# The third block of four FFN heads put into a hand-written order, with the gates moved behind the last product's splits

## The chip, the cores and the metric

The kernel runs on one core of one Trainium2 chip. The metric is the device time of one launch in microseconds (us). TensorE is PE in the profile (PEld is its weight load), VectorE is DVE, ScalarE is ACT, GpSimd is POOL, SyncE is SP. SP and POOL issue the DMAs.

## The reference

A trunk of four layers over one sequence of 512 positions and 1024 channels, all in fp32. Each layer is a mixer (S5, gated linear attention, differential attention, S5) and a SwiGLU feed-forward network (FFN), and all four FFNs have the same shape:

```python
DEPTH, D_MODEL, FFN_HIDDEN = 4, 1024, 2816
for layer in range(DEPTH):
    h = rmsnorm(x, norm_mix[layer])
    x = x + mixer(h)                      # s5, gla, diff attention, s5
    h = rmsnorm(x, norm_ffn[layer])
    g, u = split(h @ ffn_w_gate_up[layer], 2)
    x = x + (silu(g) * u) @ ffn_w_down[layer]
return rmsnorm(x, norm_final)
```

## The kernel before

**Products.** Every fp32 number is split into a high part (a cast to fp32r on ScalarE) and a low part (a subtraction on VectorE), and a product is three matmul passes: high times high, high times low, low times high. The first two matmuls of a product therefore need a low part of only one operand or of none; the third needs the low part of the weights (`seven_product`, L583 to L595). A weight piece of 512 x 256 is loaded as one DMA of 512 KB, cast by `high` (L420) and subtracted by `low` (L428).

**Blocks.** The gate and up projection of an FFN is cut into eleven blocks of 256 columns (`seven_block`, L729). A block is a 2 x 2 Strassen-like scheme with seven products of 24 matmuls each, called `one`, `two`, `three`, `four`, `five`, `six`, `seven`. Its weight pieces are named after quarters of the weight: `11`, `21`, `22`, `1` (the sum of two quarters; the second is added by an accumulating DMA on GpSimd, L759) and `3` (another such sum, the step `summed`). `add22` and `add21` (L817) add the piece 22, then 21, onto piece 1 in place; the results are called S (for `six`) and F (for `four`), and `highS`, `lowS`, `highF`, `lowF` split them. The row side (the normalised activations) has pieces of its own, formed by `total1` to `total4` (L223, L227) and split by `high1` to `high4`, `high22` and `low1` to `low22` (L236, L241).

**Outputs of a block.** `one_out`, `five_out`, `six_out` copy a PSUM bank on ScalarE; `two_out` (L803), `seven_out` (L838) and `three_out` (L845, L846) combine on VectorE. `gate1` multiplies the first half of the gate by the norm factor (L768, VectorE) and applies silu (L769, ScalarE). `four_out` does the same for the second half in a tile `g2`, multiplies it with the up half (L855) and splits both halves of the finished activation into high (L865, ScalarE) and low (L866, VectorE). Buffers: four PSUM banks for the products `a` and `c` of all blocks together, two for `d`; three buffers for the tiles `r5`, `r2`, `g2` together; three staging buffers `wst` for pieces 11 and 3 and for the pieces of w_down; five buffers `whl` for split weights.

**Order.** The instructions are traced in the order of the Python code, and a scheduler at build time arranges each engine's queue: among those that it thinks ready it takes the one traced first, and a tile's buffer is given out again only when all readers of the old tile are placed. Between `hand_all()` and `hand()` the instructions of PE, ACT, DVE, SP and POOL keep the written order among themselves; instructions traced later may still be put between them.

**The head of an FFN.** The last part of the mixer's output projection runs under `hand_all()`. The first two blocks (called a and b here, as in the code) then follow a plan, a string of steps in which `one:a` is a product or an output of a block, `add21a` or `lowFa` a step on weights, and `total3`, `high4`, `low22` a step on the row side. `planned` (L711) runs it. Layer two has a plan of its own: there the step `turn` writes x to DRAM and reads it back in another order, by four DMAs on GpSimd (L984, L986, L988, L990). After the plan `hand()` ends the written order. Then come `four_out` of a and b, then the third block (c): its five loads (`direct` for piece 11, `room1`, `room22`, `room21`, `summed`; SP, and POOL for the two sums), `one`, `five`, `add22`, `six`, and so on, left to the scheduler. Layer two traces c's loads and the split of its piece 1 ahead of `four_out` of a, and its `one` and `five` ahead of `four_out` of b. In layer 0 three blocks, in the others four, are followed by the first product with w_down (`gemm_b`, L452, matmuls L448 to L450).

In the mixer of layer two (`diff`) the last half of the output projection is written by hand too; `between` (L2779) says what is put behind which k of which row tile t. The row side's piece 3 (`total("3")`, two subtractions at L223) is formed there in the plan of layer two, right behind `one:b`; for the other layers it is formed earlier, in the mixer.

Of the kernel before, what the change touches and what calls it, by code (L numbers as in the profile page):

```python
# [17 lines left out]
ALU = mybir.AluOpType  # L18
# [7 lines left out]
NT = SEQ // P  # L26
# [314 lines left out]
class Trunk:  # L341
# [369 lines left out]
    def planned(self, plan, left, f, more):  # L711

        for step in plan.split():
            name, _, n = step.partition(":")
            if n:
                f["ab".index(n)][name]()
            elif name in more:
                more[name]()
            elif name[-1] in "ab":
                word = next(w for w in ("split", "add", "high", "low") if name.startswith(w))  # L720
                w = name[len(word) : -1]
                f["ab".index(name[-1])][word]({"S": "1", "F": "1"}.get(w, w))
            elif name in ("finish", "diag", "spread", "rows"):
                getattr(left, name)()
            else:
                word = next(w for w in ("total", "high", "low") if name.startswith(w))
                getattr(left, word)(name[len(word) :])

    def seven_block(self, fp, slots, left, wgu, b, turn, na):  # L729
# [3 lines left out]
        v = nc.vector  # L733
# [117 lines left out]

        def four_out():
            g2 = T("g2")
            scaled(g2, bank["a"], 1)
            v.tensor_tensor(keep["r5"][:], g2[:], keep["r5"][:], op=ALU.mult)  # L855
            act = fp.tile([P, 2, 2, SEQ], F32R, tag="act", name="act", bufs=na)
# [13 lines left out]
            high, low, split, direct, room21, room1, room22, summed, one, one_out, two, two_out, gate1, five, five_out,  # L870
            add, six, six_out, seven, seven_out, three, three_out, four, four_out,
        )}

    def ffn(self, l, left, after=None, turn=False, aside=None, small=None):
# [5 lines left out]
        nxt = None  # L880
        r = left.r
        with self.tc.tile_pool(name=f"ffn{l}", bufs=1, reuse_waits="tile") as fp:
# [12 lines left out]
            blocks = [self.seven_block(fp, slots, left, wgu, b, turn, na) for b in range(FFN_HIDDEN // 256)]  # L895
            f = blocks[:2]
            if glued:
# [28 lines left out]

            self.planned(plan, left, f, {"square": lambda: left.square(NT - 1, 1), "flush": self.flush, "turn": turned})
            self.hand()
            F = left.freed()
            if aside:  # L930

                self.jobs = aside(Slices(left.whole, left.g))
            else:

                self.jobs = small() if small else iter(())
                slots[:] = [F[0], F[1], slots[0], F[2], left.g[:].rearrange("p (k n) -> p k n", n=256), F[3]] + slots[1:]
            b0 = 0
            for nb in (4, 4, 3) if na == 4 else (3, 3, 3, 2):
                acts = []
                for n in range(b0, b0 + nb):  # L940
                    b = blocks[n]
                    third = l == 2 and n < 3
                    loads = lambda b: [b[w]() for w in ("direct", "room1", "room22", "room21", "summed")]
# [1537 lines left out]
    def diff(self, l, left, after):  # L2481
# [4 lines left out]
        with self.tc.tile_pool(name="diff", bufs=1) as p:  # L2486
# [289 lines left out]
            for t in range(2):  # L2776
# [73 lines left out]
```

## Time and profile before

| | |
|---|---|
| median of 3 runs | 2236.42 us (2235.76 to 2239.88) |
| profiled execution: its time | 2237.47 us |
| profiled execution: its span, first to last instruction | 2235.8 us |
| granted TensorE clock, mean | 0.998 |
| busy share of the span | PE 97%, PEld 88%, DVE 73%, ACT 51%, POOL 15% |
| DMA, mean rate | 149 GB/s |
| FFN heads in the trace (first `one:a`) | 207, 781, 1394 and 1891 us |

A row of the timeline gives the start, the duration, engine, line, operation, the tile written and the tiles read, partitions x elements, how many instructions were merged, and in brackets the idle time of the engine just before and what ended it. A product of 24 matmuls shows as one row `x24`; `x2` and `x22` are the two parts of one that waited before its third matmul. Matmul rows overlap, so a product is timed from start to start.

### The profile page before, as it was taken

Reading aid. Unit: us, or ns where it says so; the run is one execution under the profiler, and the core shown is the slowest. Engines: PE = TensorE matmul, PEld = TensorE weight load, DVE = VectorE, ACT = ScalarE, POOL = GpSimd, SP = SyncE. Lnnn points to the kernel's source line nnn. Section 1 sums busy time; section 2 is a strip of 40 time slices with the busy share of each in tenths; the row PEclk is TensorE's granted clock in tenths of the full one; section 3 lists DMA queues with packets and bytes.
Section 4 is the critical chain, followed back from the end, with each engine's and each line's share of the span. In section 5 each row is a group of like instructions: output and inputs, shape, how many; then the busy total and the mean of one; then the engine's idle time right before and its main releaser. Section 6 shows DMA issues by size and latency. Waiting matters only on the chain.

```text
span 2235.8 us, 38463 instructions
## 1 busy us (share of the span) xinstructions
PE 2172.6 (97%) x15433; PEld 1969.9 (88%) x15433; DVE 1629.2 (73%) x2497; ACT 1141.6 (51%) x1835; POOL 330.1 (15%) x441
## 2 busy tenths in 40 slices
PE   6999899999999999999999999999999999999998
PEld 5888889989988899999988888999998888989997
DVE  9965878777978597876745676967766965957675
ACT  8644535444655465564435776644544234635343
POOL 3401152430211010100002221200000001101000
PEclk9999999999999999999999999999999999999999
DMA  4357667764863576765337455975631646866532
GB/s 92 64 172 178 175 153 183 182 172 150 188 148 105 153 182 179 179 180 138 98 129 165 99 142 143 248 203 137 185 95 48 170 142 151 201 157 167 163 76 76
DMA packets 309181, 333.63 MB, mean 149 GB/s; under 512 B 70477, under 2 KB 253033, under 8 KB 308874
## 3 DMA queue, kind: packets, MB, share of 16 engines
q1 hardware_dynamic: 238970, 238.93, 35.0%
q0 software_dynamic: 70032, 92.23, 21.9%
q8 instruction: 122, 2.00, 0.4%
q14 instruction: 57, 0.47, 0.1%
HBM read 297.16 MB, written 18.75 MB: 141 GB/s over the span
## 4 chain that ended last, share of the span: by engine, by line
PE 81%; DVE 9%; ACT 4%; issue 3%; DMA 1%; SPq 1%; POOL 0%; DVEq 0%; POOLq 0%; ACTq 0%
PE a L594 20%; PE acc L448 11%; PE acc L450 11%; PE acc L449 11%; PE c L594 10%; PE d L594 5%; DVE whl L428 2%; PE y L1634 2%; PE acc L1670 2%; ACT whl L420 1%; PE op L2633 1%; PE s L2600 1%; PE tp L117 1%; PE V L1590 1%; PE acc L2688 1%
## 5 line engine op out<-in xcount | busy, mean ns | idle before, releaser
L428 DVE TENSOR_TENSOR whl<-wst,whl 128x1024 fp32r<-128x1024 f32 x260 | 316.7, 1223 | 219.9 <-ACT whl L420 216.8
L594 PE MATMUL a<-side,whl 128*128 128x256 f32 x3240 | 392.6, 277 | 6.5 <-DVE whl L428 6.3
L420 ACT CAST whl<-wst 128x1024 fp32r<-128x1024 f32 x260 | 272.1, 1051 | 244.5 <-PE acc L450 152.7
L594 PEld LDWEIGHTS a<-side,whl 128*128 128x128 f32 x3240 | 379.2, 188 | 8.7 <-DVE whl L428 7.4
L448 PE MATMUL acc<-whl,act 128*128 128x512 f32 x704 | 275.8, 392 | 3.1 <-DVE g L768 3.1
L449 PE MATMUL acc<-whl,act 128*128 128x512 f32 x704 | 274.4, 390 | 0.0
L450 PE MATMUL acc<-whl,act 128*128 128x512 f32 x704 | 274.4, 390 | 0.0
L594 PE MATMUL c<-side,whl 128*128 128x256 f32 x2160 | 261.4, 277 | 3.8 <-DVE whl L428 3.8
L594 PEld LDWEIGHTS c<-side,whl 128*128 128x128 f32 x2160 | 253.1, 188 | 4.7 <-DVE whl L428 4.6
L428 DVE TENSOR_TENSOR whl<-slot,whl 128x1024 fp32r<-128x1024 f32 x105 | 127.7, 1222 | 60.7 <-ACT whl L420 60.2
L448 PEld LDWEIGHTS acc<-whl,act 128*128 128x128 f32 x704 | 132.1, 188 | 31.5 <-DVE g L768 3.5
L450 PEld LDWEIGHTS acc<-whl,act 128*128 128x128 f32 x704 | 132.1, 188 | 27.8
L449 PEld LDWEIGHTS acc<-whl,act 128*128 128x128 f32 x704 | 132.2, 188 | 26.3
L420 ACT CAST whl<-slot 128x1024 fp32r<-128x1024 f32 x105 | 109.9, 1053 | 86.3 <-PE acc L450 46.3
L594 PE MATMUL d<-sides,whl 128*128 128x256 f32 x1080 | 132.4, 278 | 2.6 <-ACT whl L420 2.6
L594 PE MATMUL a<-sides,whl 128*128 128x256 f32 x1080 | 132.3, 278 | 2.2 <-DVE whl L428 1.2
L594 PEld LDWEIGHTS d<-sides,whl 128*128 128x128 f32 x1080 | 128.0, 188 | 3.4 <-ACT whl L420 3.4
L594 PEld LDWEIGHTS a<-sides,whl 128*128 128x128 f32 x1080 | 127.9, 188 | 3.5 <-DVE whl L428 1.4
L428 DVE TENSOR_TENSOR whl<-halves,whl 128x1024 fp32r<-128x1024 f32 x87 | 105.9, 1221 | 32.1 <-ACT whl L420 31.8
L420 ACT CAST whl<-halves 128x1024 fp32r<-128x1024 f32 x87 | 91.0, 1052 | 71.6 <-DVE halves L817 24.9
L759 POOL DMA_DIRECT2D wst<-in_ffn_w_gate_up_dram x44 | 57.1, 1297 | 453.3 <-DMA wst<-in_ffn_w_gate_up_dram 167.5
L865 ACT CAST act<-r 128x512 fp32r<-128x512 f32 (+1 forms) x110 | 66.2, 643 | 107.7 <-DVE r L846 85.7
(511 smaller groups left out, 4028.9 us busy)
## 6 DMA issues: line engine op xcount, KB each, us to landing
wst<-in_ffn_w_gate_up_dram SPq DMA_DIRECT2D x88, 512.0 KB, 4.7
wst<-in_ffn_w_down_dram SPq DMA_DIRECT2D x88, 512.0 KB, 4.6
slot<-in_ffn_w_gate_up_dram SPq DMA_DIRECT2D x69, 512.0 KB, 6.3
wst<-in_ffn_w_gate_up_dram POOLq DMA_DIRECT2D x44, 512.0 KB, 6.0
halves<-in_ffn_w_gate_up_dram SPq DMA_DIRECT2D x42, 512.0 KB, 6.1
wst<-in_s_w_glu_dram SPq DMA_DIRECT2D x32, 512.0 KB, 4.9
wst<-in_diff_w_qkv_dram SPq DMA_DIRECT2D x24, 512.0 KB, 4.7
slot<-in_ffn_w_gate_up_dram POOLq DMA_DIRECT2D x18, 512.0 KB, 9.1
```

Source lines behind the costliest of these rows:

```text
L117: tr.nc.tensor.transpose(p[:, j], h[:, j * P : (j + 1) * P], tr.ident[:])
L420: self.last["high"] = self.nc.scalar.copy(hl[:, 0], w[:])
L428: self.last["low"] = self.nc.vector.tensor_tensor(hl[:, 1], w[:], hl[:, 0].bitcast(F32), op=ALU.subtract)
L448: mm(out, lh, rh, start=first, stop=False)
L449: mm(out, lh, rl, start=False, stop=False)
L450: self.last["mm"] = mm(out, ll, rh, start=False, stop=last)
L594: mm(o, *two, start=first and not (j or k or n), stop=k == 3 and n == 2, skip_group_check=True,)
L759: nc.gpsimd.dma_start(w[:], left.quarter(*plus, b), accum_op=ALU.add)
L865: self.last["act high"] = nc.scalar.copy(dst[:, 0, j], src[:, j])
L1590: mm(V[kk][z][:, bs(b)], inm[:, z, bs(b)], U[:, bs(b)], start=True, stop=True)
L1634: mm(yb[:, b], q[:, j, b], om[:, j // 2, bs(b)], start=False, stop=j == 3)
L1670: mm(accs[t][:], zT[:, m // 2, kk, t * P : (t + 1) * P], hl[:, m % 2, kk % 2], start=kk == 0 and m == 0, stop=kk == KT - 1 and m == 2,)
```

## The change

Four edits, all of them to the order:

1. In the plan of layers 0, 1 and 3 the splits for `four` (`high22`, `add21`, `low22`, `highF`, `lowF`) come ahead of the gates; `gate1:a` now follows `add21b` and `highFb`, and `gate1:b` and both `three_out` leave the plan. In layer two's plan `gate1:b` and both `three_out` leave too.
2. A second plan for all layers, still in the written order: the loads and first products of block c, with the outputs of a and b between them. `hand()` comes behind it. `four_out` becomes three steps: `gate2`, `times` and `parts`; `parts` (the splits of the finished activation) is traced after that plan.
3. The special case of layer two for block c is gone.
4. `total3` leaves layer two's plan; it is formed in `diff`, behind k = 3 of the last row tile.

No instruction is added or removed.

```diff
@@ planned
-                f["ab".index(n)][name]()
+                f["abc".index(n)][name]()
@@ seven_block
-        def four_out():
-            g2 = T("g2")
-            scaled(g2, bank["a"], 1)
-            v.tensor_tensor(keep["r5"][:], g2[:], keep["r5"][:], op=ALU.mult)
+        def gate2():
+            keep["g2"] = T("g2")
+            scaled(keep["g2"], bank["a"], 1)
+
+        def times():
+            v.tensor_tensor(keep["r5"][:], keep["g2"][:], keep["r5"][:], op=ALU.mult)
+
+        def parts():
             act = fp.tile([P, 2, 2, SEQ], F32R, tag="act", name="act", bufs=na)
...
@@ ffn
-            f = blocks[:2]
+            f = blocks[:3]
...
             if l == 2:
                 plan = """
-                    split21a one:a split21b square flush one:b total3 total1 one_out:a finish high1 low1 total2 split1a
+                    split21a one:a split21b square flush one:b total1 one_out:a finish high1 low1 total2 split1a
...
-                    high22 low22 three:a add21a highFa add21b lowFa highFb three:b lowFb seven_out:b gate1:a four:a gate1:b
-                    four:b three_out:a three_out:b
+                    high22 low22 three:a add21a highFa add21b lowFa highFb three:b lowFb seven_out:b gate1:a four:a
+                    four:b
                 """
             else:
...
-                    six_out:b total4 split22a high4 low4 seven:b seven_out:a split22b three:a seven_out:b gate1:a gate1:b
-                    add21a high22 low22 three:b highFa add21b lowFa highFb lowFb four:a four:b three_out:a three_out:b
+                    six_out:b total4 split22a high4 low4 seven:b seven_out:a split22b three:a seven_out:b high22 add21a
+                    low22 highFa lowFa three:b add21b highFb gate1:a lowFb four:a four:b
                 """
...
+            def loads(b=blocks[2]):
+                for w in ("direct", "room1", "room22", "room21", "summed"):
+                    b[w]()
...
-            self.hand()
             F = left.freed()
...
+            plan = """
+                loads split11c three_out:a split1c one:c gate2:a one_out:c five:c add22c highSc times:a gate1:b lowSc
+                five_out:c three_out:b gate2:b times:b
+            """
+            self.planned(plan, left, f, more)
+            self.hand()
...
-                    third = l == 2 and n < 3
...
-                    if third and n == 0:
-                        loads(blocks[2])
-                        blocks[2]["split"]("1")
-                    if third and n == 1:
-                        for step in ("one", "one_out", "five", "five_out"):
-                            blocks[2][step]()
-                        blocks[2]["add"]("22")
-                        blocks[2]["split"]("1")
-                    if n > 1 and not third:
+                    if n > 2:
...
-                        b["four"]()
-                    acts.append(b["four_out"]())
+                        for step in ("four", "gate2", "times"):
+                            b[step]()
+                    acts.append(b["parts"]())
@@ diff
-                3: {1: (one,), 3: (one,), 5: (one,)},
+                3: {1: (one,), 3: (one, lambda: nxt[0].total("3")), 5: (one,)},
```

More of the change, by code (lines that the diff above doesn't have):

```diff
@@ L715, in planned @@
             if n:
-                f["ab".index(n)][name]()
+                f["abc".index(n)][name]()
             elif name in more:
                 more[name]()
-            elif name[-1] in "ab":
+            elif name[-1] in "abc":
                 word = next(w for w in ("split", "add", "high", "low") if name.startswith(w))
                 w = name[len(word) : -1]
-                f["ab".index(name[-1])][word]({"S": "1", "F": "1"}.get(w, w))
+                f["abc".index(name[-1])][word]({"S": "1", "F": "1"}.get(w, w))
             elif name in ("finish", "diag", "spread", "rows"):
@@ L870, in seven_block @@
             high, low, split, direct, room21, room1, room22, summed, one, one_out, two, two_out, gate1, five, five_out,
-            add, six, six_out, seven, seven_out, three, three_out, four, four_out,
+            add, six, six_out, seven, seven_out, three, three_out, four, gate2, times, parts,
         )}
@@ L925, in turned @@
                 r = self.turn_x(left.r) if turn else r
-            self.planned(plan, left, f, {"square": lambda: left.square(NT - 1, 1), "flush": self.flush, "turn": turned})
-            self.hand()
+            def loads(b=blocks[2]):
+                for w in ("direct", "room1", "room22", "room21", "summed"):
+                    b[w]()
+            more = {"square": lambda: left.square(NT - 1, 1), "flush": self.flush, "turn": turned, "loads": loads}
+            self.planned(plan, left, f, more)
             F = left.freed()
@@ L936, in ffn @@
                 slots[:] = [F[0], F[1], slots[0], F[2], left.g[:].rearrange("p (k n) -> p k n", n=256), F[3]] + slots[1:]
+            plan = """
+                loads split11c three_out:a split1c one:c gate2:a one_out:c five:c add22c highSc times:a gate1:b lowSc
+                five_out:c three_out:b gate2:b times:b
+            """
+            self.planned(plan, left, f, more)
+            self.hand()
             b0 = 0
```

1 line of the change is left out of this document (removed).

## The prediction

> **What bounds the kernel now.** I read the page first: the busy shares, then the chain that ended last.
>
> ```profile
> PE 2172.6 (97%) x15433; PEld 1969.9 (88%) x15433; DVE 1629.2 (73%) x2497; ACT 1141.6 (51%) x1835; POOL 330.1 (15%) x441
> PE 81%; DVE 9%; ACT 4%; issue 3%; DMA 1%; SPq 1%; POOL 0%; DVEq 0%; POOLq 0%; ACTq 0%
> ```
>
> TensorE has work nearly all the time, so an edit that only reorders can give no more than the idle time of PE that it removes. Next I read PE's timeline through the four FFN heads. Layer one's, from the first matmul of `four:a`:
>
> ```profile
> 815.21 0.39 PE L594 MATMUL a<-side,whl 128*128 128x256 f32 x2
> 817.34 5.50 PE L594 MATMUL a<-side,whl 128*128 128x256 f32 x46 [1.74 <-DVE whl L428]
> 822.67 2.88 PE L594 MATMUL a<-sides,whl 128*128 128x256 f32 x24
> ...
> 826.89 2.78 PE L594 MATMUL c<-side,whl 128*128 128x256 f32 x22 [1.11 <-DVE whl L428]
> ...
> 830.66 0.50 PE L594 MATMUL d<-sides,whl 128*128 128x256 f32 x2 [0.44 <-ACT whl L420]
> 831.00 2.84 PE L594 MATMUL a<-side,whl 128*128 128x256 f32 x22
> 833.67 2.73 PE L594 MATMUL d<-sides,whl 128*128 128x256 f32 x22
> 836.24 2.88 PE L594 MATMUL a<-side,whl 128*128 128x256 f32 x24
> 838.96 2.88 PE L594 MATMUL c<-side,whl 128*128 128x256 f32 x24
> ```
>
> A product that waits for nothing takes 838.96 - 836.24 = 2.72 us (0.1133 a matmul). From 815.21 to 836.24 stand six (`four:a`, `four:b`, `one:c`, `five:c`, `six:c`, `two:c`): 6 x 2.72 = 16.32 us of work in 21.03. So 4.71 us are lost: 1.74 in `four:a` and 1.11 in `five:c`, each for a low part after two matmuls, 0.44 at `two:c`, and the rest in slower matmuls just behind each wait. The other heads:
>
> ```profile
> 243.37 5.51 PE L594 MATMUL a<-side,whl 128*128 128x256 f32 x46 [1.73 <-DVE whl L428]
> 276.88 0.50 PE L448 MATMUL acc<-whl,act 128*128 128x512 f32 x1 [3.08 <-DVE g L768]
> ...
> 1406.64 5.68 PE L594 MATMUL c<-side,whl 128*128 128x256 f32 x46 [0.51 <-DVE whl L428]
> 1413.41 2.86 PE L594 MATMUL a<-side,whl 128*128 128x256 f32 x22 [0.76 <-DVE whl L428]
> 1444.68 0.51 PE L594 MATMUL d<-sides,whl 128*128 128x256 f32 x2 [1.30 <-ACT whl L420]
> 1450.69 0.40 PE L594 MATMUL c<-side,whl 128*128 128x256 f32 x2
> ...
> 1927.32 5.50 PE L594 MATMUL a<-side,whl 128*128 128x256 f32 x46 [1.74 <-DVE whl L428]
> ```
>
> Layers 0 and 3 repeat layer one; layer 0 also waits at the start of its first product with w_down. Layer two waits early (`five:a`, `six:a`) and in block c. What PE waits for is VectorE's queue, in layer one:
>
> ```profile
> 810.86 1.29 DVE L768 TENSOR_TENSOR r<-r,R 128x512 f32<-128x512 f32 x2
> ...
> 816.06 2.50 DVE L428 TENSOR_TENSOR whl<-lent,whl 128x1024 fp32r<-128x1024 f32 x2
> ...
> 819.08 1.22 DVE L428 TENSOR_TENSOR whl<-wst,whl 128x1024 fp32r<-128x1024 f32 x1
> ...
> 822.61 0.68 DVE L866 TENSOR_TENSOR act<-r,act 128x512 fp32r<-128x512 f32 x1
> ...
> 825.62 1.22 DVE L428 TENSOR_TENSOR whl<-halves,whl 128x1024 fp32r<-128x1024 f32 x1
> ...
> 829.70 1.22 DVE L428 TENSOR_TENSOR whl<-halves,whl 128x1024 fp32r<-128x1024 f32 x1 [0.52 <-ACT whl L420]
> 830.84 1.22 DVE L428 TENSOR_TENSOR whl<-slot,whl 128x1024 fp32r<-128x1024 f32 x1
> ...
> 854.39 1.23 DVE L428 TENSOR_TENSOR whl<-wst,whl 128x1024 fp32r<-128x1024 f32 x1 [1.55 <-ACT whl L420]
> ```
>
> These are both gates, `lowFa` and `lowFb`, the low parts of c's pieces 11 and 1, then `lowS` and the low part of 21. Activation splits (L866), which nothing needs until w_down, stand ahead of them. From start to start a 1024-element operation takes 1.14 us (829.70 to 830.84); two 512-element ones in 1.29 make about 0.60 each. VectorE has slack only later (1.55 us at 854.39). On ScalarE a cast takes 0.95 from start to start:
>
> ```profile
> 816.26 1.04 ACT L420 CAST whl<-lent 128x1024 fp32r<-128x1024 f32 x1 [1.55 <-DVE lent L817]
> 817.21 1.04 ACT L420 CAST whl<-wst 128x1024 fp32r<-128x1024 f32 x1
> ...
> 1918.30 1.28 ACT L769 ACT_TABLE_LOAD   x1
> ```
>
> **The change part by part**, first in layer one. *The gates behind the last splits.* VectorE reaches the old place of the gates at 810.86. Now it does `add21a` to 812.0, `low22` to 813.1, `lowFa` to 814.3, `add21b` to 815.4 and `gate1:a` to 816.0; ScalarE casts F of b by 816.5, and `lowFb` is done at 817.7. `four:a` starts at 815.21 as before and asks for `lowFa` at 815.44: the 1.74 us go. `four:b` ends at 815.21 + 5.44 = 820.65, not 822.67.
>
> *Block c in written order.* The silu of `gate1:a` now stands ahead of c's first cast on ScalarE: 817.1, cast to 818.1, low part of 11 to 819.3, `three_out:a` to 820.5. `one:c` needs a PSUM bank that the first half of `three_out:a` frees (819.9), so it starts at 820.65. The low part of 1 is ready at 821.7, and `five:c` (823.37) no longer waits. Then `gate2:a` to 822.3, `add22c` to 823.4, `times:a`, `gate1:b` to 824.6. The cast of S stands behind `one_out:c`, which waits for the end of `one:c`: it runs from 823.95 to 825.0, and `lowS` is done at 826.2 to 826.3. `six:c` (826.09) asks for it at 826.3: at most 0.1 lost. `six:c` ends at about 828.9.
>
> *Activation splits later.* What is late next is the low part of 21 for `two:c`. Behind `lowS` VectorE has `three_out:b` (1.2) and `gate2:b` (0.6). `gate2:b` needs one of three buffers, and the next one comes free when `parts` of a has read `r5`: one split (0.6). A second split, of b, is ready and traced earlier than c's piece 21 (0.6). So 3.0 us behind 826.3 the low part starts, and it is ready at 830.5; `two:c` would ask at 829.2. Its last 22 matmuls end at 830.5 + 22 x 0.1133 = 833.0, with the ramp 833.1, instead of 836.24: **3.1 us gained**. Bounds: with `times:b` and a further split ahead too (1.2) the gain is 1.9; with nothing ahead it is the whole 4.71. The splits pushed back are covered by the slack from 850 on. If that were gone, each would cost its 0.6.
>
> [...]
>
> *Layers 3 and 0.* Here the activation table is loaded (1.28 us) ahead of the first silu, now in front of c's first cast. Of 1.28 some 0.7 is spare, since the low part of 11 (819.3) is asked for at 820.9 and `three_out:a` frees the bank 0.7 before `one:c`; 0.6 is lost: **2.5** in layer 3. In layer 0 the wait of 3.08 stands behind a transfer of w_down:
>
> ```profile
> 273.92 1.04 ACT L420 CAST whl<-wst 128x1024 fp32r<-128x1024 f32 x1 [5.87 <-DMA wst<-in_ffn_w_down_dram]
> ```
>
> A PSUM bank is freed by c's second gate at 276.14, which VectorE has queued behind the split of that piece. If the transfer lands when it did, the wait grows by all that the head gave: 0. If its buffer comes free earlier with the queue, all 2.5 stay; if the two swap places on VectorE, 3.08 more go. I take **1.5**, as the buffers are freed by steps that move up by some 2 us.
>
> *Layer two.* `total3` goes from 1399.23 to the mixer's last row tile:
>
> ```profile
> 1399.23 1.29 DVE L223 TENSOR_TENSOR s<-halves 128x512 f32<-128x512 f32 x2
> ```
>
> It lies ahead of the last residual add there and delays that by about half its 1.2 us, so of the early waits (0.51 + 0.76) about 0.6 goes. Against this stands GpSimd's queue. There `turn` comes ahead of c's loads in the written order, while before the sum for piece 1 was put between its DMAs:
>
> ```profile
> 1413.52 1.29 POOL L759 DMA_DIRECT2D halves<-in_ffn_w_gate_up_dram  x1 [9.42 <-DMA halves<-in_ffn_w_gate_up_dram]
> ...
> 1414.85 1.35 POOL L988 DMA_DIRECT2D rturn<-rcol  x1
> 1431.16 0.56 POOL L990 DMA_DIRECT2D rturned<-rturn  x1 [14.96 <-DMA rturn<-rcol]
> ...
> halves<-in_ffn_w_gate_up_dram POOLq DMA_DIRECT2D x1, 512.0 KB, 5.8
> ...
> halves<-in_ffn_w_gate_up_dram POOLq DMA_DIRECT2D x1, 512.0 KB, 10.8
> ```
>
> Now the sum waits behind L990, that is until 1429 to 1432, and lands 5.8 to 10.8 us later (the two sums into `halves` issued at 1413.52 and 1439.01): 1435 to 1443. `five:c` asks for the low part of 1 at about 1439.0, so the sum should land by 1436.7; the middle, 1439, costs 2.3 us on ScalarE, VectorE and PE alike, as all three queues are written by hand there. Without it block c would end 0.7 us ahead of 1450.69. Bounds: 1.3 gained, 1.6 lost at 1439 (4.5 at the late end). I take **0**. [...]
>
> Sum: 3.1 + 2.5 + 1.5 + 0 = 7.1 us. The profiled execution took 2237.47, 1.05 above the median of the runs shown; the waits are differences within it, so I take the sum off the median: 2236.42 - 7.1 = **2229.3 us**.
>
> **The rivals.**
>
> *All of it goes* (chance 0.12): the scheduler lets c's splits pass the activation splits. 4.71 + 4.1 + 4.1 in layers one, 3 and 0, and 2 in layer two: 15, or 2221. For it: nothing needs these splits for 20 us. Against: in the trace the scheduler put one at 822.61, ahead of the low part at 825.62 that PE waited for.
>
> *VectorE is the bound* (0.22): the waits only move to `two:c`. The same operations have to pass VectorE before the low part of 21, whatever their order: 1.9 in layer one, 1.3 in layer 3, nothing in 0 and two: 3.2 less, 2233.2, within what a measurement can tell from no change (0.2%, 4.5 us). For it: VectorE's row at 829.70 is its only wait in ten us.
>
> *Transfers held by the written order* (0.16), slower: SP now issues c's piece 3 behind the load into a freed slot.
>
> ```profile
> 803.69 1.84 SPq L409 DMA_DIRECT2D wst<-in_ffn_w_gate_up_dram  x2
> ...
> 807.43 0.37 SPq L756 DMA_DIRECT2D slot<-in_ffn_w_gate_up_dram  x1
> ...
> 807.84 1.28 POOL L759 DMA_DIRECT2D wst<-in_ffn_w_gate_up_dram  x1 [12.36 <-DVE whl L428]
> ...
> wst<-in_ffn_w_gate_up_dram POOLq DMA_DIRECT2D x1, 512.0 KB, 11.0
> ```
>
> That is 807.8 instead of 803.69, 4.1 us later, and its accumulating DMA goes from 807.84 to about 812, landing at 823 in layer one. It is asked for by about 831 (`two:c` ends at 833.1; a cast and a split come before), so 8 us are to spare. If a sum of the fourth block gets in front on GpSimd, a landing is added, and each us beyond 831 stops PE at `seven:c` in all four heads. From 1.8 us late the gain is gone; at 3 us, 4 x 3 - 7.1 = 5 us slower, 2241. Against it: the spare time, which is shorter only in layer two, where the sums wait for `turn`.
>
> **How the numbers follow.** My forecast has a chance of 0.50 (its own range, from the bounds above, 2225 to 2232), and that of the rivals 0.12, 0.22 and 0.16. The range takes in the first rival whole, the second, and half of the third: **2220 to 2239**. Faster by over 0.2%: 0.50 + 0.12 = 0.62; within: 0.22; slower: 0.16.
>
> **What would show it.** Right: in layers 0, 1 and 3 no wait in `four:a`, none in `five:c`, one of about 1.3 us at `two:c`; L768 behind both `add21` on VectorE; the first L866 behind `lowS`. The wait of 3.08 in layer 0 between 0 and 5. In layer two L990 ahead of the sum for piece 1 on GpSimd. Wrong: a wait in `one:c` or `six:c` of over 0.5 us, which would mean that the written order waits where the scheduler did not; a wait for a DMA at `seven:c`; or PE gaining in the heads and losing it behind them.

## The result, and the profile after

The changed kernel takes 2245.71 us (median of 6 runs, 2243.07 to 2246.86), the kernel before on the same chip 2236.45 (6 runs, 2233.49 to 2239.88). The ratio is 1.0037, with a 95% interval of 1.0025 to 1.0050: slower by 9 us, where 7 us faster was predicted. The profiled execution took 2246.86, its span is 2245.1, its mean granted clock 0.995. Lines of the functions in the heads are the old ones up to L850, then shifted by 2 to 5: the activation splits are L869 (ScalarE) and L870 (VectorE), `times` is L857, `turn`'s transfers are L989 to L995. The busy shares of the page:

```profile
PE 2180.7 (97%) x15433; PEld 1976.8 (88%) x15433; DVE 1629.1 (73%) x2497; ACT 1139.8 (51%) x1835; POOL 330.2 (15%) x441
```

The same 15433 matmuls cost TensorE 8.1 us more (2180.7 for 2172.6). They ran slower, then, in a few places; why is shown below. The head of layer one in TensorE's timeline:

```profile
818.87 5.74 PE L594 MATMUL a<-side,whl 128*128 128x256 f32 x48
824.45 2.99 PE L594 MATMUL a<-sides,whl 128*128 128x256 f32 x24
827.27 2.99 PE L594 MATMUL c<-side,whl 128*128 128x256 f32 x24
830.86 0.51 PE L594 MATMUL a<-side,whl 128*128 128x256 f32 x2 [0.59 <-ACT whl L420]
832.12 2.78 PE L594 MATMUL a<-side,whl 128*128 128x256 f32 x22 [0.76 <-DVE whl L428]
```

`four:a` and `four:b` are one row of 48 without a wait, and `five:c` waits for nothing: both as predicted. New are two waits in `six:c`, 0.59 for the cast of S and 0.76 for its low part. What stands ahead of them on VectorE and ScalarE:

```profile
828.48 1.28 DVE L870 TENSOR_TENSOR act<-r,act 128x512 fp32r<-128x512 f32 x2
830.84 1.23 DVE L428 TENSOR_TENSOR whl<-halves,whl 128x1024 fp32r<-128x1024 f32 x1 [1.07 <-ACT whl L420]
```

```profile
829.27 0.59 ACT L796 COPY r<-a 128x512 f32<-128x512 f32 x1 [0.66 <-DVE act L870]
829.75 1.05 ACT L420 CAST whl<-halves 128x1024 fp32r<-128x1024 f32 x1
```

The tile `r1` has two buffers. `one_out:c` (L796) writes a third `r1`, so it waits until block a's is split (L870), and the cast of S stands behind `one_out:c` on ScalarE. The splits that were to come later were pulled ahead of `lowS` by that buffer. Layer 3 has the same two waits in `six:c` and one more ahead of them; rows of TensorE, ScalarE and VectorE:

```profile
1941.50 3.07 PE L594 MATMUL a<-sides,whl 128*128 128x256 f32 x24 [0.71 <-DVE r L845]
...
1948.45 0.50 PE L594 MATMUL a<-side,whl 128*128 128x256 f32 x2 [1.06 <-ACT whl L420]
1949.71 2.78 PE L594 MATMUL a<-side,whl 128*128 128x256 f32 x22 [0.76 <-DVE whl L428]
```

```profile
1936.63 1.28 ACT L769 ACT_TABLE_LOAD   x1
1937.92 0.63 ACT L769 ACTIVATE r<-r 128x512 f32<-128x512 f32 x1
1938.46 1.03 ACT L420 CAST whl<-wst 128x1024 fp32r<-128x1024 f32 x1
```

```profile
1939.53 1.22 DVE L428 TENSOR_TENSOR whl<-wst,whl 128x1024 fp32r<-128x1024 f32 x1 [1.66 <-DMA halves<-in_ffn_w_gate_up_dram]
```

The load of the gates' table (1.28) and the silu stand ahead of the cast of c's piece 11; its low part waits 1.66 (the row names a DMA, but ScalarE's cast ended at 1939.49), `three_out:a` behind it is late, and `one:c` waits 0.71 for the bank. With 0.82 at `two:c` the waits of this head add up to 3.35 us, for 1.35 in layer one.

In layer 0 the predicted wait of 3.08 for w_down is gone, but another takes its place in the operators that the next mixer prepares during that product:

```profile
285.47 0.68 PE L1392 MATMUL xps<-ident,halves 64*64 64x64 f32 x16 [3.66 <-DVE halves L1247]
```

The old wait of 3.08 is not the same in every execution. In the run with only the sum for operand three moved (the last of the experiments but one), whose edit leaves layer 0 as it was, it is 1.10.

Layer two is where most was lost. GpSimd, ScalarE, VectorE and TensorE, then TensorE's clock in two stretches (start and end; length, then busy time of PE, PEld, DVE, ACT, POOL, the granted clock, DMA share, GB/s):

```profile
1415.61 0.57 POOL L991 DMA_DIRECT2D x<-xturn  x1 [9.92 <-issue]
...
1429.76 0.56 POOL L995 DMA_DIRECT2D rturned<-rturn  x1 [12.80 <-DMA rturn<-rcol]
1430.31 1.37 POOL L759 DMA_DIRECT2D halves<-in_ffn_w_gate_up_dram  x1
```

```profile
1442.32 1.04 ACT L420 CAST whl<-halves 128x1024 fp32r<-128x1024 f32 x1 [6.44 <-DMA halves<-in_ffn_w_gate_up_dram]
```

```profile
1443.40 1.23 DVE L428 TENSOR_TENSOR whl<-halves,whl 128x1024 fp32r<-128x1024 f32 x1 [4.93 <-ACT whl L420]
...
1447.48 2.19 DVE L870 TENSOR_TENSOR act<-r,act 128x256 fp32r<-128x256 f32 x4
```

```profile
1445.38 5.19 PE L594 MATMUL c<-side,whl 128*128 128x256 f32 x24 [4.42 <-DVE g L768]
...
1457.01 4.34 PE L594 MATMUL d<-sides,whl 128*128 128x256 f32 x22 [2.19 <-DVE whl L428]
```

```profile
1440.00:1445.00 5.00, 0.95 (x9) 0.75 (x7) 1.60 (x2) 2.05 (x3) 1.27 (x1) 0.83 1.14 301
1445.00:1450.00 5.00, 4.62 (x22) 4.66 (x23) 4.68 (x8) 3.09 (x5) 0.00 (x0) 0.50 1.17 266
```

The sum for piece 1 is issued at 1430.31 instead of 1413.52, and the cast that waits for it starts at 1442.32; everything behind it in VectorE's written order (`gate2:a`, `add22c`, four activation splits, `lowS`) is late too. The wait of `five:c` names `gate2:a` (L768), which frees its bank and stands right behind the split of piece 1. TensorE stands still for 4.42 us, its granted clock falls to 0.50, and `five:c` takes 5.19, where it took 2.99 in layer one.

Reading the starts of the same products in both traces gives what each head gained or lost, from its first `one:a` to the first product of its second group of blocks (316, 909, 1522 and 2018 us in the trace of before). The table has the profiled executions of most experiments too; minus is gained, in us:

| kernel | layer 0 | layer 1 | layer 2 | layer 3 |
|---|---|---|---|---|
| predicted | -1.5 | -3.1 | 0 | -2.5 |
| changed | +0.9 | -2.1 | +7.5 | -0.6 |
| GpSimd free in the second plan | +0.4 | -1.0 | +7.5 | -0.6 |
| SyncE and GpSimd free in layer two | +1.0 | -2.5 | +1.8 | -0.6 |
| layer two as before | +0.6 | -1.6 | -0.1 | -0.6 |
| the same, table loaded early | -3.5 | -0.9 | -0.1 | -1.5 |
| the same, highSc ahead of one_out:c too | -5.8 | -2.0 | -0.1 | -3.6 |
| gates moved, nothing else | +2.2 | +0.5 | +0.6 | +1.5 |
| written order, gates not moved, layer two as before | -2.8 | -2.2 | 0.0 | -2.7 |
| sum for operand three moved, nothing else | -1.9 | +0.6 | -0.1 | -0.7 |

The last row has the old order in layers 0, 1 and 3, so its figures there are what one profiled execution differs from another by. Kernels with the same order in a head differ by up to 1.9 in layer 0, 1.6 in layer 1 and 0.7 in layer 3, and by 0.1 in layer two where it is as before. Smaller differences are not read; the changed kernel's +0.9 and -0.6 in layers 0 and 3 are such, and say only that the predicted gain did not come. A part of this scatter is TensorE's clock (1.5 us in one head of layer 0, last section). In the changed kernel the four heads sum to +5.7. Nearly all else of its 9.3 arose where the order is the same: 1.4 in the first 26 us (most other profiles lack it), 1.6 in layer one's mixer (see the end) and 0.8 in layer two's mixer.

### The profile page after: what moved, and what is told of

Same layout as the page of the kernel before. It is cut to its first block, busy times and chain, and to the rows that moved or that the text cites. A ratio compares the mean times of both kernels' runs of the same rounds, so it can differ in the third digit from the quotient of the medians.

```text
span 2245.1 us, 38438 instructions
## 1 busy us (share of the span) xinstructions
PE 2180.7 (97%) x15433; PEld 1976.8 (88%) x15433; DVE 1629.1 (73%) x2497; ACT 1139.8 (51%) x1835; POOL 330.2 (15%) x441
## 5 line engine op out<-in xcount | busy, mean ns | idle before, releaser
L869 ACT CAST act<-r 128x512 fp32r<-128x512 f32 (+1 forms) x110 | 66.4, 644 | 100.7 <-DVE r L846 84.7
```

The lines of the kernel that those rows point to most:

```text
L869: self.last["act high"] = nc.scalar.copy(dst[:, 0, j], src[:, j])
```

## The experiments

All ratios are to the kernel before on the same chip, with the 95% interval. Of the long lines of the plans only the steps that matter are shown.

### Layer two: which queue

First the changed kernel with GpSimd left out of the written order of the second plan:

```diff
+            E = mybir.EngineType
+            self.hand(E.PE, E.Activation, E.DVE, E.SP)
             self.planned(plan, left, f, more)
```

> The changed kernel with GpSimd left out of the written order in the second plan (block c's part); the scheduler then puts the sum for piece 1 of layer two's block c between turn's first and second transfer, where the kernel before has it, and every other engine keeps the written order. Theory (the loss is that sum waiting behind turn's four transfers): it is issued near 1414 and lands before 1427, the wait of 4.42 of five:c and those of 2.19 and 0.76 behind it shrink to under 2 in all, and the time falls by 5 to 8 us from 2245.7, to 2238-2241. Rival (the loss in layer two is the written order on VectorE and ScalarE itself): the sum lands early but layer two stays as long, 2244-2246.

2244.77 us, ratio 1.0039 (1.0026 to 1.0051). The sum for piece 1 was issued early, as wanted, and `five:c`'s wait went; the time stayed. Rows of GpSimd, SyncE and TensorE:

```profile
1413.59 1.28 POOL L759 DMA_DIRECT2D halves<-in_ffn_w_gate_up_dram  x1 [9.90 <-DMA halves<-in_ffn_w_gate_up_dram]
...
1438.02 1.31 POOL L759 DMA_DIRECT2D wst<-in_ffn_w_gate_up_dram  x1 [6.00 <-DVE halves L817]
```

```profile
1405.06 16.52 SPq L756 DMA_DIRECT2D halves<-in_ffn_w_gate_up_dram  x2
...
1422.76 1.11 SPq L409 DMA_DIRECT2D wst<-in_ffn_w_gate_up_dram  x2
```

```profile
1455.24 0.58 PE L594 MATMUL c<-side,whl 128*128 128x256 f32 x1 [4.06 <-DVE whl L428]
```

A second transfer was behind the first. SyncE's row of two loads into freed slots spans 16.5 us, as the second waits for its slot, and piece 3 (`wst`) is written behind them: 1422.76, where the kernel before issued it at 1419.26. Its sum goes out at 1438.02 (before: 1432.13), and the split that needs it stops TensorE for 4.06. So the theory held for one wait and fell as the whole cause: with SyncE's queue still in the written order and GpSimd's no longer, layer two loses the whole 7.5. Then both queues were freed, in layer two alone:

```diff
+            E = mybir.EngineType
+            if l == 2:
+                self.hand(E.PE, E.Activation, E.DVE)
```

> The changed kernel with, in layer two only, both SyncE and GpSimd left out of the written order of the second plan; TensorE, ScalarE and VectorE keep it. SyncE's load of piece 3 then stands ahead of the load that waits for a slot, and on GpSimd the sum for piece 1 stands between turn's transfers and the sum for piece 3 ahead of turn's last. Theory (layer two loses to two transfers held by the written order, one on each queue, and freeing GpSimd alone only moved the wait from five:c, 4.42, to the product of piece 3, 4.06): no wait of TensorE over 1.5 between 1430 and 1460, the granted clock stays at 1.00 there, and layer two costs within 1 of before; the time is 2235-2238, as with layer two put back. Rival (VectorE's written order in layer two costs by itself): 2240-2243, with waits for VectorE in their place.

2238.29 us, 1.0012 (1.0004 to 1.0021): layer two's loss falls from 7.5 to 1.8. TensorE's longest wait there with the product behind it, and the sum for piece 3 on GpSimd:

```profile
1448.56 0.38 PE L594 MATMUL c<-side,whl 128*128 128x256 f32 x1 [1.69 <-DVE whl L428]
1448.98 4.55 PE L594 MATMUL a<-side,whl 128*128 128x256 f32 x24
```

```profile
1430.00 1.30 POOL L759 DMA_DIRECT2D wst<-in_ffn_w_gate_up_dram  x1 [15.91 <-DVE r L838]
```

Three quarters of the loss are the two queues together. 1.8 is left, as the rival said, but smaller, and the expected clock of 1.00 did not come: behind the wait of 1.69 the next 24 matmuls take 4.55 us at a granted clock of 0.50 (1449 to 1452 us), where 24 take 2.88 at 1.00 (layer one of the kernel before, 822 to 826 us): 1.67 more, about as much as is left. Whether the written order of the other engines costs anything beyond that wait is open. A run with SyncE alone freed is not on record, so the share of GpSimd by itself is not shown. As a control, layer two wholly as before:

> The changed kernel with layer two alone put back as it was before (old plan, block c's steps written in the loop, the sum for operand three in the plan); layers 0, 1 and 3 keep the change. Theory (layer two lost 8.3, layers 1 and 3 gained 1.5 and 0.6, layer 0 lost 0.8; what arose at the start and in the mixer of layer one, where the order of instructions is the same, is chance): 2234-2237, not slower than before. Rival (the 1.4 at the start and the 1.5 in the mixer of layer one come with the change): 2238-2239. Second rival (layer two is not where the time went): above 2241.

2237.57 us, 1.0004 (0.9995 to 1.0013). Layer two explains some 8 us; and layers 0, 1 and 3, where 7 were predicted, gain nothing measurable together. How much of the stop is the halved clock? 22 matmuls that compute nothing (they show as 44 in the trace) were written into it:

```diff
-                one:c gate2:a one_out:c five:c add22c
+                one:c gate2:a one_out:c fill five:c add22c
```

> The changed kernel with 22 matmuls that compute nothing (identity by identity, 128x128) written ahead of five:c in layer two, where TensorE stands still for 4.42; the transfers stay as late as they are. Theory (the stop itself costs; the halved clock behind it, 0.50 for 5 us, is mostly hidden because six:c waits for VectorE's lowSc anyway): the clock stays at 1.00 there, five:c takes 3.0 for 5.2, six:c begins at the same time, and the time falls by 0 to 2 from the changed kernel, 2243.5-2245.7. Rival (the halved clock is a good part of the loss): five:c, six:c and two:c all move up, and the time falls by 3 to 5, 2240.5-2242.5.

2244.29 us, 1.0036 (1.0024 to 1.0048); layer two lost 7.2.

```profile
1443.45 3.07 PE L594 MATMUL c<-side,whl 128*128 128x256 f32 x24
1448.35 0.50 PE L594 MATMUL a<-side,whl 128*128 128x256 f32 x2 [1.82 <-ACT whl L420]
1449.61 4.30 PE L594 MATMUL a<-side,whl 128*128 128x256 f32 x22 [0.76 <-DVE whl L428]
```

`five:c` takes 3.07 for 5.19, and `six:c` waits all the longer. The halved clock of `five:c` was hidden behind ScalarE and VectorE; the lateness is what counts. The slow matmuls came all the same, one product later: 22 of `six:c` take 4.30 behind waits of 1.82 and 0.76, for 2.78 in the changed kernel, and 4.30 is what 22 take at a granted clock of 0.50 with layer two as before (last section). So this run does not price the halved clock of the whole stretch. (The filler also changed the order of some later operations, so the run is read for these rows.)

### Layers 0, 1 and 3: what ate the gain

The r1 half of block a split early, to free the buffer:

```diff
-                one:c gate2:a one_out:c five:c
+                one:c gate2:a half:a one_out:c five:c
...
```

> The changed kernel with the r1 half of block a's finished activations (its split into two parts) written into the second plan right behind gate2:a, ahead of one_out:c; all else as changed. Theory (one_out:c waits for one of the two buffers of r1, and gives it up late, because the scheduler puts the split of block a behind gate1:b): the waits at the head of six:c (0.59 and 0.76 in layer 1, 1.06 and 0.76 and 0.82 in layers 0 and 3) fall under 0.5 in all for each head, and the time falls by 2 to 5 us, to 2240.5-2243.5. Rival (the next operand of six:c, highSc and lowSc behind add22c, is as late as the buffer): the waits change their releaser and not their length, 2245-2246.

2244.09 us, 1.0036 (1.0024 to 1.0049). With GpSimd freed as well:

> The edits of the two runs before it together: GpSimd free in the second plan, and the r1 half of block a split right behind gate2:a. Theory: the two gains add, 7 to 12 us below the changed kernel, 2234-2238, which is level with the kernel before or faster by up to 2. Rival (in layer two both remove the same wait): no faster than the better of the two alone, 2238-2241.

2241.87 us, 1.0023 (1.0014 to 1.0032): layer two still lost 7.4, and whether the two differ is within the noise. In layer one the first of them has

```profile
823.95 0.50 PE L594 MATMUL a<-side,whl 128*128 128x256 f32 x2 [0.45 <-ACT whl L420]
825.21 2.77 PE L594 MATMUL a<-side,whl 128*128 128x256 f32 x22 [0.76 <-DVE whl L428]
...
828.75 2.81 PE L594 MATMUL d<-sides,whl 128*128 128x256 f32 x22 [0.53 <-DVE whl L428]
```

1.74 of waits instead of 1.35: the split itself stands in the way of `add22c` on VectorE. By its waits the rival held, though the time lies between the two ranges; freeing the buffer by doing its reader earlier is no gain. A rewritten plan with all of VectorE's urgent work first (layer two as before; `gate1:a` also leaves the first plan, and `half` is the early split of the last two runs):

```diff
-                loads split11c three_out:a split1c one:c gate2:a one_out:c five:c add22c highSc times:a gate1:b lowSc
-                five_out:c three_out:b gate2:b times:b
+                loads split11c gate1:a three_out:a half:a split1c one:c gate2:a add22c one_out:c five:c highSc lowSc times:a
+                gate1:b five_out:c three_out:b gate2:b times:b
...
```

> Layer two as before; in layers 0, 1 and 3 the second plan rewritten so that VectorE does first what TensorE waits for: gate1:a behind split11c, the r1 half of block a split ahead of one:c, the sum of operand S and its split ahead of times:a and gate1:b. Theory (in these heads VectorE's order sets the waits that replaced the gain): one:c's wait (0.7 to 0.8 in layers 0 and 3) and six:c's two (1.3 to 1.8 in each head) fall to under 0.8 in each head in all; layers 1 and 3 gain 1 to 2 each over the run with layer two alone put back, layer 0 gains nothing at its end since its down product waits for its weights; 2232-2235. Rival (VectorE has no slack there whatever its order): the waits return at two:c or three:c, 2236-2238.

2244.00 us, 1.0031 (1.0020 to 1.0041), not the 2232 to 2235 expected: `six:c` is served, `five:c` waits 1.0 to 1.2 instead, and the later steps (`gate2:b`, the last split of a) come so late that `six_out:c` (L828), which ScalarE does behind them, stops the next product. Layers 0 and 1:

```profile
262.63 4.61 PE L594 MATMUL a<-side,whl 128*128 128x256 f32 x24 [3.08 <-ACT r L828]
...
841.21 3.09 PE L594 MATMUL a<-side,whl 128*128 128x256 f32 x24 [3.08 <-ACT r L828]
```

The move of the gates alone, from the kernel before:

```diff
-                    seven_out:b gate1:a gate1:b
-                    add21a high22 low22 three:b highFa add21b lowFa highFb lowFb four:a four:b three_out:a three_out:b
+                    seven_out:b high22 add21a
+                    low22 highFa lowFa three:b add21b highFb gate1:a lowFb four:a four:b gate1:b three_out:a three_out:b
```

> The kernel before with the first part of the change alone, in layers 0, 1 and 3: the splits of the last operands stand ahead of the gates in the plan; block c's first products, the finished activations and all of layer two are as before. Theory (the wait of 1.73 in four:a goes, and of it about half comes back at one:c and six:c, because VectorE does the gates later): layers 1 and 3 gain 0.5 to 1.5 each, 2234-2236. Rival (all of the 1.7 comes back because VectorE is the bound): no difference, 2236-2237.

2244.79 us, 1.0041 (1.0029 to 1.0053): by itself this edit loses as much as the whole change. Layer 3, TensorE and VectorE:

```profile
1941.80 4.38 PE L594 MATMUL a<-sides,whl 128*128 128x256 f32 x22 [3.82 <-DVE whl L428]
```

```profile
1939.33 0.68 DVE L768 TENSOR_TENSOR g<-a,R 128x512 f32<-128x512 f32 x1
1939.93 0.68 DVE L866 TENSOR_TENSOR act<-r,act 128x512 fp32r<-128x512 f32 x1
1940.53 1.22 DVE L428 TENSOR_TENSOR whl<-wst,whl 128x1024 fp32r<-128x1024 f32 x1
```

`four:a` no longer waits, but gates and activation splits then pass VectorE ahead of the low part of c's piece 11, and `one:c` waits 3.82. The other edit by itself is the written order (with the later activation splits), the gates where they were and layer two as before:

```diff
-                    seven_out:b high22 add21a low22 highFa lowFa three:b add21b highFb gate1:a lowFb four:a four:b
+                    seven_out:b gate1:a gate1:b add21a high22 low22 three:b highFa add21b lowFa highFb lowFb four:a four:b
...
-                add22c highSc times:a gate1:b lowSc
+                add22c highSc times:a lowSc
```

> Layer two as before; in layers 0, 1 and 3 block c's first products in the written order and the later split of the finished activations, but both gates where the kernel before has them, ahead of the last splits. Theory (moving the gates alone costs 3 to 4 a head because it makes block c's first splits late, and the written order is what pays that back; without the move of the gates the order has only the waits of 1.10 and 0.45 to gain): four:a keeps its 1.7, the waits at five:c and six:c fall under 0.6 in all, 2234.5-2237. Rival (the written order by itself gains the most, and the move of the gates only costs): 2231-2234.

2229.61 us, 0.9972 (0.9961 to 0.9982). The rival held, and by more than it said. The written order alone gains some 7 us, with the wait in `four:a` still there and none over 0.3 behind it up to the down product:

```profile
813.76 5.50 PE L594 MATMUL a<-side,whl 128*128 128x256 f32 x46 [1.74 <-DVE whl L428]
819.10 2.88 PE L594 MATMUL a<-sides,whl 128*128 128x256 f32 x24
```

So of the two edits the moved gates alone give 1.0041, the written order alone 0.9972, and both together, with layer two as before, 1.0004. Two cheap edits were then tried on that last kernel: a table load in a stretch where ScalarE is idle, and two steps put back in the order, `one_out:c` behind `highSc` and `gate1:b` behind `lowSc`.

```diff
-                    seven_out:b high22 add21a
+                    seven_out:b high22 load add21a
...
+            def silu():
+                if glued:
+                    one = self.sp.tile([P, 1], F32, tag="ms", name="ms", bufs=2)
+                    self.nc.scalar.activation(one[:], self.mhalf[:, :1], AF.Silu)
...
-                loads split11c three_out:a split1c one:c gate2:a one_out:c five:c add22c highSc times:a gate1:b lowSc
+                loads split11c three_out:a split1c one:c gate2:a five:c add22c highSc times:a one_out:c lowSc gate1:b
```

> Layer two as before; in layers 0, 1 and 3 the change with two edits: ScalarE splits operand S (highSc) ahead of one_out:c and VectorE splits it (lowSc) ahead of gate1:b, so that six:c no longer stands behind the wait for r1's buffer; and in layers 0 and 3 one ScalarE operation on a single column loads the table of the gates in a stretch where ScalarE is idle. Theory (the waits at one:c and six:c come from ScalarE's and VectorE's order): one:c's 0.71 to 0.80 in layers 0 and 3 goes, six:c's two waits (1.3 in layer 1, 1.8 in layers 0 and 3) fall to under 0.7 in all; layers 1 and 3 gain 1 to 2.5 each over the run with layer two alone put back, layer 0 nothing at its end: 2233-2235.5. Rival (the two parts of VectorE's work exceed what TensorE needs in that stretch, whatever comes first): the wait moves to two:c or seven:c, 2236.5-2239.

2226.31 us, 0.9954 (0.9942 to 0.9967): faster than both kernels, by 10 and 19 us. The gates are moved here, and yet from `four:a` to `two:c` none of these heads waits over 0.3; one wait of 0.98 is left, at `seven:c`:

```profile
826.50 3.09 PE L594 MATMUL a<-side,whl 128*128 128x256 f32 x24 [0.98 <-ACT r L828]
```

Which edit did it? The table load alone:

> Layer two as before; layers 0, 1 and 3 as changed, with the early table load alone: in layers 0 and 3 one ScalarE operation on a single column takes the load of the gates' table (1.28) into a stretch where ScalarE is idle, ahead of the splits; the order of highSc and one_out:c is the changed kernel's. Theory (in layers 0 and 3 the change's late gates put the table load ahead of block c's first split, and that, not the order, is what those two heads lost): layer 1 stays as with layer two alone put back, layers 0 and 3 gain 2 to 3 each, 2231-2234. Rival (the order of ScalarE around r1's buffer is what counts, and the table load only shifts the wait): 2235.5-2238, six:c's waits in layers 0 and 3 unchanged.

2231.68 us, 0.9977 (0.9968 to 0.9986). ScalarE's load now lies at 1914.61, and `one:c` in layers 0 and 3 waits no more, while `six:c` keeps its two waits:

```profile
1914.61 1.28 ACT L934 ACT_TABLE_LOAD   x1
```

```profile
1932.54 0.51 PE L594 MATMUL a<-side,whl 128*128 128x256 f32 x2 [0.89 <-ACT whl L420]
```

Behind these two waits the other 22 matmuls take 4.37 to 4.39 us in all three heads, for 2.78 in the changed kernel; with layer two as before 22 took 4.30 at a granted clock of 0.50 (last section), so this is by estimate the clock too. So each edit gives about half: 0.27% the table, 0.23% the order, and in the profiled executions a good part of the second is these slow matmuls, some 1.6 us in each of the three heads. In layer 0 the gains are larger than the waits removed in the head (the transfers and the small operators of the down product move up as well); why so much was not separated. Last, the sum for operand three:

```diff
-                    split21a one:a split21b square flush one:b total3 total1 one_out:a
+                    split21a one:a split21b square flush one:b total1 one_out:a
...
-                3: {1: (one,), 3: (one,), 5: (one,)},
+                3: {1: (one,), 3: (one, lambda: nxt[0].total("3")), 5: (one,)},
```

> The kernel before with the move of the sum for operand three alone (layer two's two subtractions of 128x512 go from the plan into the loop of the products before it). Theory: the wait of 0.51 in layer two at 1406.64 goes or shrinks and nothing else moves but one transfer of GpSimd, which changes places with turn's last; 0 to 1 faster than before, 2235.5-2236.4. Rival (VectorE is needed in that loop for the evacuation of the banks): 0.5 to 2 slower.

2235.43 us, 0.9992 (0.9983 to 1.0001): unclear. The wait of 0.51 in layer two is gone from the trace, as predicted, but the whole head is only 0.1 shorter (last row of the table).

> The fastest version so far (layer two's plan as before, highSc ahead of one_out:c, the table load early) with the move of layer two's sum for operand three added. Theory (that move is worth 0.51 in layer two and nothing else): 0 to 1 below the version without it, 2225-2226.5. Rival (its gain was chance): 2226-2227.5.

2227.38 us, 0.9956 (0.9944 to 0.9969), no different from the version without it. What the move costs or gains stays below what these runs resolve.

## Why the prediction was wrong, step by step

The step that failed most is layer two's, taken at 0 where 7.5 us were lost. In layers 0, 1 and 3 the sum booked a gain for which other steps paid.

**Layer two (taken 0, measured +7.5).** The mechanism on GpSimd was right, L990's counterpart ahead of the sum, but it was priced too low. By the prediction's own figures a landing at 1439 costs 1.6 us and one at 1443 some 5.6 (it says 4.5); 0 was taken. The sum landed by 1442.3, the late end of the range given (1435 to 1443). Two more things were left out. SyncE's side was worked out for layer one, as the slower rival, where it has 8 us to spare; it was not worked out for layer two, where the text itself says that the spare time is shorter. There it is enough for the whole loss: with GpSimd freed and SyncE not, 7.5 stayed. And "costs on ScalarE, VectorE and PE alike" took the delay once, while on VectorE 6.9 us pass from the start of the low part of 1 to that of `lowS`.

**The gates behind the last splits ("the 1.74 us go").** They went, in layers 0, 1 and 3. But the sum booked them as a gain, and in the run with this edit alone 3.82 come back at `one:c` in layers 0 and 3. That looks like the rival "VectorE is the bound", which got 0.22, but the rival has it that the waits move whatever the order, and the fastest version shows otherwise: with the gates moved, the table loaded early and two steps put back, no wait over 0.3 is left up to `two:c`, though VectorE is busy without a pause there (10.00 us of the ten from 820 to 830). What failed is the order that the sum took as harmless, not the amount of VectorE's work.

**Layer one ("at most 0.1 lost" in `six:c`).** Measured 0.59 + 0.76. The step counted the buffers of `g2`, but not the two of `r1`; the sign that was named, the first activation split behind `lowS`, came out the other way (828.48 against 830.84). By luck the total of the waits, 1.35, is what the prediction had at `two:c` (1.3), where none came. The rest of the miss is in its rate: products without a wait took 2.8 to 3.0 us from start to start here, where the sum had 2.72; why is not shown. Head: -2.1 for -3.1 predicted.

**The table load ("some 0.7 is spare, 0.6 is lost").** The waits of layer 3's head are 2.0 us longer than layer one's (3.35 for 1.35), and with the table loaded early they are 1.65 (0.89 + 0.76): the load cost some 2 us of waits and not 0.6. The 0.7 of spare time was read off the schedule worked out for layer one; in the trace `one:c` waits 0.71 for the bank. Measured: layer 3 gained 0.6 for 2.5 predicted, layer 0 lost 0.9 where 1.5 was to be gained. Loading the table early gives layer 3 another 0.9, with 22 slow matmuls in `six:c` (4.37 us for 2.78), and layer 0 some 4.

**Layer 0's wait for w_down.** It is gone, within the 0 to 5 given, and the next thing was late: 3.66 at the small operators. The 3.08 that the sum started from was itself one execution's figure (1.10 in another with the same order).

**Right:** no wait in `four:a`, and in layers 0, 1 and 3 none in `five:c`; the wait of 0.51 that the moved sum takes out of layer two, though the run with that move alone shows no gain in time for it; a wait of over 0.5 in `one:c` or `six:c` was named as the sign that the written order waits where the scheduler did not, and that is what the trace shows.

## What to carry to other kernels

A step that moves behind a wait takes its whole queue along (here the sum for piece 1, from 1413.52 to 1430.31): before fixing an order by hand, list for every engine, the two that issue transfers first, what each new neighbour waits for, and do so in the stage with the least spare time. Count all buffers that a written order reuses, since a buffer's last reader is pulled forward and the order meant is not the order got (here L870 at 828.48, ahead of `lowS` at 830.84). Where an engine is busy nearly all the time, moving its work away from one wait only pays if the work lands where nothing waits for what stands behind it; a table load (1.28 us here) is such work, and one operation on a single column places it (it gave 0.27%).

## What the runs showed of the hardware

**The granted clock was 0.50 behind some stops, and 1.00 behind others of the same length.** Behind a stop of 4.42 us in layer two of the changed kernel it was 0.50 (1445 to 1450 us); around one of 3.08 in layer 0 of the kernel before it was 1.00 (270 to 285 us). In the rewritten plan the same stop of 3.08 stands in layer 0 and layer 1: behind it 24 matmuls took 4.61 us in one and 3.09 in the other. Shorter stops show both as well. In layer 0 of the changed kernel `six:c` waits 1.06 and 0.76 with two matmuls between, and the next 22 take 2.78 (granted clock 1.00 from 255 to 262 us). The same waits with layer two as before (granted clock 0.50 from 257 to 259 us):

```profile
254.34 0.50 PE L594 MATMUL a<-side,whl 128*128 128x256 f32 x2 [1.06 <-ACT whl L420]
255.61 4.30 PE L594 MATMUL a<-side,whl 128*128 128x256 f32 x22 [0.76 <-DVE whl L428]
```

So a wait of this size does not always cost its own length alone: here it cost 1.5 us more in one execution and nothing more in another. What decides between the two was not shown. The 12 runs of the rewritten plan go from 2235.76 us, at a mean granted clock of 0.998, to 2247.10 at 0.995.

**A product behind 32 tiny matmuls took 4.58 and 4.93 us in two profiles and 2.98 in a third.** In layer one's mixer 32 matmuls of two columns run without a break, and the product behind them takes 4.58 us before (granted clock 0.58 from 640.5 to 644.5 us), 2.98 with layer two as before, and 4.93 in the changed kernel (0.55 from 643.9 to 648.4 us), where the tiny ones are slow too (4.90 for 3.63); the order is the same in all three. Whether the tiny matmuls are the cause was not shown. Kernel before, changed kernel, layer two as before (one fence each):

```profile
640.37 4.58 PE L594 MATMUL a<-whl,side 128*128 128x256 f32 x24
```

```profile
639.06 4.90 PE L2296 MATMUL dps<-ind,la 128*128 128x2 f32 x32
643.82 4.93 PE L594 MATMUL a<-whl,side 128*128 128x256 f32 x24
```

```profile
640.57 2.98 PE L594 MATMUL a<-whl,side 128*128 128x256 f32 x24
```

Between these profiles the stretch to 660 us differs by 1.6 us a step. A single profile can gain or lose that without any part in the change.
